# A diffusion block's mixture of experts: large experts' first products from split weights, the other experts' sums ahead of the last weights, the last two experts joined by products

## The chip, the cores and the metric

One core of a Trainium2 chip runs the whole kernel in one launch. The metric is device time in microseconds (us) of an execution. Where a text names an engine: PE is TensorE, DVE is VectorE, ACT is ScalarE, POOL is GpSimd, and SP is SyncE, which here only issues transfers.

## The reference, cut

512 latent tokens of width 1024 and 256 context tokens pass one layer: a mixer (neighbourhood attention and a gated DeltaNet, merged), then a mixture of experts, then a last RMSNorm. The change lies almost wholly in the second half:

```
logits = xf @ w_router + b_router                 # xf: 512 x 1024, modulated RMSNorm of x
top_val, top_idx = top_k(logits, 4)               # 4 of 32 experts for a token
gates = softmax(top_val)
...
hb = xb @ w1[e] + b1[e]                           # w1[e]: 1024 x 2048
gate, up = hb[:, :1024], hb[:, 1024:]
gate = minimum(gate, 7); up = clip(up, -7, 7)
act = (up + 1) * gate * sigmoid(1.702 * gate)
y = act @ w2[e] + b2[e]                           # w2[e]: 1024 x 1024
...
x = x + g2 * sum over the 4 experts of gate * y
out = rmsnorm(x, final_norm_w)
```

Everything is float32. The weights of the experts are 32 x 12 MB (of 2^20 bytes), each read once.

## The kernel before, in words

The first 727 us or so are the mixer. Its projections already work with split operands: a helper (lines 29 and 30 of the profile) copies a float32 tile on ACT to fp32r as the high part and subtracts it on DVE for the low part, and three fp32r products (lines 981, 982 and 984: high by high, low by high, high by low) stand for one in fp32.

For the experts, the router counts each expert's tokens, `order` ranks the experts by count into the row `eint`, and the experts are then worked through by rank. A large one has 128 slots for tokens, a small one 64; with 64 slots the two halves of the 1024 output columns are worked on side by side by the two halves of TensorE's columns. Expert 0 and 1 are large and fixed (their indices are known without the ranking), then even ones are large and odd ones small; the last two, 30 and 31, are small. Tokens beyond an expert's slots go to `overflow`, a loop under a condition at the end, which has nothing to do with these inputs; its condition still joins all engines.

`Stream` loads the weights in 1 MB chunks of 128 partitions x 2048 columns on SP's queue, in a fixed order: for each e the four chunks "g" (gate half of w1) of e, the four of w2 of e - 1, and the four "u" (up half) of e. There are RAWB buffers of the tile "raw"; `pump` issues loads as long as there is room and, beyond the fixed experts, only once `eint` is there.

The loop follows the same order. `mm` makes the products of one such group in fp32 (line 481; one fp32 product of 128x512 shows as two records) and adds the bias by a product (lines 491 and 494). `gate` and `up` make the activation from PSUM on DVE and ACT, `transp` turns it by products with the identity (line 228), `weighted` (line 539) multiplies w2's result by gates and g2, and `scatter` (line 528) writes its rows by an indirect DMA to the DRAM tensor y4d, which has four rows for each token. `fetch` (line 220) loads a later expert's token rows from h2d by an indirect DMA, and `gather` turns them. Experts 0 and 1 get their rows by one-hot products in `slots`. `places` and `overflow_table` make the tables of tokens, rows and gates by one-hot products.

```
def mm(x, e, kind, after=None):
    ...
    for c in range(4):
        r = stream.take(e, kind, c)
        for j in range(2):
            ...
                nc.tensor.matmul(o[n], x[:, k, 0:m], r[:, j, 512 * n:512 * n + 512], ...)
        stream.pump()
```

The tail, after the condition's join: y4d is loaded in 8 transfers of 1 MB (line 84) into the same buffers; DVE (line 611) and POOL (line 621) add them into x1; expert 31's result is added by products with a one-hot matrix (line 706), with the second bias (line 703); squares on ACT (line 713), inverse roots on POOL and DVE, and the stores (line 720).

The order of instructions on an engine is the scheduler's: by the order of the program, but work that is ready can be put ahead, unless `keep_in_program_order` holds it.

Of the kernel before, what the change touches and what calls it, by code (L numbers as in the profile page):

```python
# [18 lines left out]
RAWB = 14  # L19
FIXED = 2  # L20
# [18 lines left out]
class Stream:  # L39
# [3 lines left out]
    def __init__(self, tc, ctx, w1, w2, y4d, NE):  # L43
# [15 lines left out]
        self.tail = False  # L59
# [12 lines left out]
    def pump(self, most=RAWB, behind=None):  # L72
        while self.loaded < min(self.used + most, len(self.order) if self.tail else self.last):
# [21 lines left out]
def small(e):  # L95

    return e >= 30 or e > 1 and e % 2 == 1


def column(e):  # L100

    if e < FIXED:
        return e
    return 61 - e if e >= 30 else 16 + (e - 3) // 2 if e % 2 else e // 2 + 1
# [38 lines left out]
def moe(tc, ctx, cst, release, rps, rt, rtp, h2, hx, h2d, x1d, modd, w1, b1, w2, b2, fn_d, out, NE=32):  # L143
# [5 lines left out]
    y4d = dr.tile([2048, 1024], F32, name="y4d")  # L149
# [4 lines left out]
    pctx = ExitStack()  # L154
    ident, iot, iot1, pcol, ones1 = cst["ident"], cst["iota"], cst["iota1"], cst["pcol"], cst["ones_row"]
    mx, E, cnt = rt.mx, rt.E, rt.cnt

# [36 lines left out]
    def slots():  # L194

        oh = xp.tile([128, 4, 256], F32R, name="yy", bufs=2)
        v = oh.rearrange("p t (a s) -> p t a s", a=2)
        for t in range(4):
            nc.vector.tensor_tensor(v[:, t], iot1[:, None, :].to_broadcast([128, 2, 128]),
                                    rt.pp[:, t, 0:2, None].to_broadcast([128, 2, 128]), op=OP.is_equal)  # L200
        for e in range(2):
            XT[e] = xp.tile([128, 8, 128], F32, name="xt", bufs=3)
        for q in range(4):
            p = bank("tr")
            for b in range(2):
                for i in range(2):
                    for t in range(4):
                        nc.tensor.matmul(p[:, 256 * b:256 * b + 256], h2[i][:, t, 256 * q + 128 * b:256 * q + 128 * b + 128], oh[:, t, :],
                                         start=b == 0 and i == 0 and t == 0, stop=b == 1 and i == 1 and t == 3)
            p = p.rearrange("p (b e s) -> p b e s", b=2, e=2)  # L210
            nc.scalar.activation(XT[0][:, 2 * q:2 * q + 2], p[:, :, 0], AF.Copy)
            nc.vector.tensor_copy(XT[1][:, 2 * q:2 * q + 2], p[:, :, 1])
# [10 lines left out]

    def turn(e, src, q, dst):

        p = bank("tr").rearrange("p (k s) -> p k s", k=4)
        for k in range(4):
            nc.tensor.transpose(p[:, k, :], src[:, (4 * q + k) * 128:(4 * q + k + 1) * 128], ident)  # L228
        if small(e):
            nc.scalar.activation(dst.rearrange("p (n k) s -> p k n s", n=2), p.rearrange("p k (n s) -> p k n s", n=2), AF.Copy)  # L230
        else:
            nc.scalar.activation(dst[:, 4 * q:4 * q + 4], p, AF.Copy)  # L232
# [5 lines left out]
    def gather(e):  # L238
        XT[e] = xp.tile([128, 8, 128], F32, name="xt", bufs=3)
        if small(e):  # L240
            XT[e] = XT[e][:, 0:4].rearrange("p a (b s) -> p (a b) s", b=2)
        turned(e, xg[:, e % 4], XT[e])
# [8 lines left out]
    def order(get):  # L251

        cmp = get([128, 32, 32], BF, 1)
        nc.vector.tensor_scalar(kb, iot[:, 0:32], -1.0, 31.0, op0=OP.mult, op1=OP.add)
        nc.vector.memset(kb[:, 0:1], 1.0e6)
        nc.vector.memset(kb[:, 1:2], 9.0e5)
# [19 lines left out]
    tlast = sb.tile([128, 4], F32, name="tlast")  # L276
# [7 lines left out]
    nc.sync.dma_start(g2b, dap(modd, 3072, [[0, 128], [1, 1024]]))  # L284
    for n in range(2):
        nc.sync.dma_start(g2s[64 * n:64 * n + 64, :], dap(modd, 3072 + 512 * n, [[0, 64], [1, 512]]))
# [36 lines left out]
    def sums(get, pl, sel, n):  # L323

        oh = get([128, 16, 128], BF, 0)
        for i in range(16):
            nc.gpsimd.tensor_scalar(oh[:, i], iot1, pl[:, i:i + 1], None, op0=OP.is_equal)
        rh = get([128, 16, 5, n], BF, 1)
        nc.gpsimd.tensor_tensor(rh[:, :, 0, :], sel, iot[:, 1:17, None].to_broadcast([128, 16, n]), op=OP.mult)
        nc.vector.tensor_scalar(rh[:, :, 1, :], sel, pcol, None, op0=OP.mult)  # L330
        for i in range(3):
            nc.gpsimd.tensor_tensor(rh[:, :, 2 + i, :], sel, gp[:, i, :, None].to_broadcast([128, 16, n]), op=OP.mult)
        return oh, rh

    get = scratch()
    slots()
    order(get)
# [7 lines left out]
    def places():  # L345
# [17 lines left out]
        nc.gpsimd.tensor_tensor(tmp.rearrange("p (t k) e -> p t k e", k=4), E.rearrange("p (t k) e -> p t k e", k=4),  # L363
# [4 lines left out]
        def finish():  # L368
# [9 lines left out]
            nc.vector.tensor_copy(tlast[:, 0:1], toks[:, column(NE - 1):column(NE - 1) + 1])  # L378
# [86 lines left out]
    BS = {}  # L465


    def mm(x, e, kind, after=None):
# [6 lines left out]
        m = 64 if s else 128  # L475
        for c in range(4):
            r = stream.take(e, kind, c)
            for j in range(2):
                k = 2 * c + j
                for n in range(2):  # L480
                    nc.tensor.matmul(o[n], x[:, k, 0:m], r[:, j, 512 * n:512 * n + 512], start=k == 0, stop=w2_ and k == 7)  # L481
            stream.pump()
            if after:
                after(c)
        if not w2_:
            i = 0 if kind == "g" else 1
            if s:
                if kind == "g":
                    BS[e] = wk3.tile([128, 2, 64], F32R, name="bsel", bufs=2)
                    nc.scalar.activation(BS[e], selr[:, :, k0:k0 + 1].to_broadcast([128, 2, 64]), AF.Copy)  # L490
                nc.tensor.matmul(p[0], BS[e].rearrange("p n s -> p (n s)"), bb[:, i], start=False, stop=True)  # L491
            else:
                for n in range(2):
                    nc.tensor.matmul(p[n], selr[:, n, k0:k0 + 1].to_broadcast([128, 128]), bb[:, i], start=False, stop=True)  # L494
# [4 lines left out]
    def gate(e, p):  # L499
        s = wk3.tile([128, 1024], F32, name="sg", bufs=2)  # L500
        for n, b in enumerate(p):
            v = slice(512 * n, 512 * n + 512)
            nc.vector.tensor_scalar(b, b, 7.0, None, op0=OP.min)  # L503
            nc.scalar.activation(s[:, v], b, AF.Sigmoid, scale=1.702)  # L504
            nc.vector.tensor_tensor(s[:, v], s[:, v], b, op=OP.mult)
        GS[e] = s

    def up(e, p):
        s = GS.pop(e)
        for n, b in enumerate(p):  # L510
            v = slice(512 * n, 512 * n + 512)
            nc.vector.tensor_scalar(b, b, 7.0, -7.0, op0=OP.min, op1=OP.max)  # L512
            nc.vector.scalar_tensor_tensor(s[:, v], b, 1.0, s[:, v], op0=OP.add, op1=OP.mult)
        AT[e] = s

    def transp(e):
# [3 lines left out]
        turned(e, AT.pop(e), t)  # L520
        TA[e] = t
# [12 lines left out]
    def weighted(e, p):  # L534
        y = xp.tile([128, 1024], F32, name="yy", bufs=2)
        k = column(e)
        for n, b in enumerate(p):
            v = slice(512 * n, 512 * n + 512)
            nc.vector.scalar_tensor_tensor(y[:, v], b, gates[:, k:k + 1], g2s if small(e) else g2b[:, v], op0=OP.mult, op1=OP.mult)  # L539
        return y[:, 0:512] if small(e) else y  # L540

    def overflow(n, ovi, rowd, gatd):

        with tc.If(n > 0):
            with tc.For_i(0, n) as j:
                e = nc.values_load(ovi[0:1, bass.ds(j, 1)], min_val=0, max_val=31)
                with ExitStack() as s2:
# [57 lines left out]
                    nc.gpsimd.indirect_dma_start(out=y4d[:, :], out_offset=bass.IndirectOffsetOnAxis(ap=rw[:, 0:1], axis=0),  # L605
                                                 in_=y, in_offset=None, bounds_check=2047, oob_is_err=False)

    Y4 = {}

    def add(t, y_, v=slice(0, 1024)):  # L610
        tc.keep_in_program_order(nc.vector.tensor_tensor(x1[:, t, v], x1[:, t, v], y_, op=OP.add))  # L611

    def others(t, c):

        Y4[t, c] = r = stream.take(t, "y", c)
        if t == 3 and c == 0:
# [1260 lines left out]
```

## Time and profile before

| | |
|---|---|
| three runs | 1869.14, 1871.02, 1864.0 us; median 1869.14 |
| the profiled execution | 1867.78 us, its span in the trace 1866.0 us |
| mean granted TensorE clock of it | 0.978 |
| PE busy | 1748.1 us, 94% of the span |
| DVE, ACT, POOL busy | 687.6, 395.4, 267.5 us |
| moved by DMA | 566.05 MB, 303 GB/s over the span |

The span goes from the first to the last record of the trace; 1.8 us of the execution lie around it. A clock of 1.00 in a window is 2.4 GHz, 0.50 is 1.2 GHz. "DMA share" is the mean busy share of the 16 transfer engines.

### The profile page before, as it was taken

How to read it: one execution, taken by the hardware profiler on the slowest of the kernel's cores; microseconds unless marked ns; L12 is line 12 of the kernel's file. 1: busy time of each engine (PE TensorE's matmuls, PEld its weight loads, DVE VectorE, ACT ScalarE, POOL GpSimd, SP SyncE). 2: the span in 40 equal slices, each digit the busy share in tenths (PEclk: the TensorE clock that was granted, in tenths of full speed). 3: DMA queues.
4: the chain of work that ended last, by engine and by line, in shares of the span. 5: the costliest groups of instructions: out<-in, count | busy, mean ns of one | idle time of the engine just before them, and what ended most of it. 6: DMA issues, size and time to landing. Idle time of an engine off the chain costs nothing. (4 is left out here: it accounts for less than half of the span.)

```text
span 1866.0 us, 23887 instructions
## 1 busy us (share of the span) xinstructions
PE 1748.1 (94%) x9003; PEld 955.9 (51%) x9003; DVE 687.6 (37%) x1356; ACT 395.4 (21%) x718; POOL 267.5 (14%) x321
## 2 busy tenths in 40 slices
PE   5979899899989898999999999999999999999984
PEld 1556677777867776444444444444444444444331
DVE  2456796964558766511111111111111111111125
ACT  2534446342246432100000100000000000010001
POOL 0131101433000532340000000000000000000005
PEclk9989899999989998999999999999999999999997
DMA  7647649755785735999999999999999999999995
GB/s 255 206 126 231 206 120 244 185 146 145 190 204 159 241 106 195 394 408 390 373 397 387 406 384 385 403 387 380 400 387 381 389 395 378 375 394 378 404 373 225
DMA packets 263451, 566.05 MB, mean 303 GB/s; under 512 B 61521, under 2 KB 124453, under 8 KB 263204
## 3 DMA queue, kind: packets, MB, share of 16 engines
q1 hardware_dynamic: 186568, 491.26, 72.1%
q10 hardware_dynamic: 69885, 57.00, 10.6%
q0 software_dynamic: 6880, 16.24, 2.3%
q8 instruction: 72, 1.18, 0.3%
q14 instruction: 46, 0.38, 0.1%
HBM read 529.16 MB, written 43.16 MB: 307 GB/s over the span
## 5 line engine op out<-in xcount | busy, mean ns | idle before, releaser
L481 PE MATMUL h<-raw,xt 128*64 128x512 f32 (+1 forms) x2048 | 684.4, 596 | 5.2 <-DMA raw<-in_w_dram 5.0
L481 PEld LDWEIGHTS h<-raw,xt 128*64 128x64 f32 (+1 forms) x2048 | 259.3, 163 | 366.6 <-issue 361.5
L481 PE MATMUL y<-raw,at 128*64 128x512 f32 (+1 forms) x1024 | 338.0, 598 | 0.3 <-ACT at L232 0.3
L481 PEld LDWEIGHTS y<-raw,at 128*64 128x64 f32 (+1 forms) x1024 | 132.6, 164 | 187.7 <-issue 185.5
L981 PE MATMUL pj<-hh,whi 128*128 128x512 f32 (+3 forms) x432 | 163.3, 380 | 7.7 <-ACT zb L1166 3.4
L982 PE MATMUL pj<-hl,whi 128*128 128x512 f32 (+3 forms) x432 | 160.7, 375 | 0.0
L984 PE MATMUL pj<-hh,wlo 128*128 128x512 f32 (+3 forms) x432 | 158.6, 376 | 0.0
L503 DVE TENSOR_SCALAR h<-h 128x512 f32<-128x512 f32 x48 | 31.9, 696 | 314.1 <-PE h L494 207.6
L512 DVE TENSOR_SCALAR h<-h 128x512 f32<-128x512 f32 x48 | 31.9, 696 | 294.8 <-PE h L494 198.8
L30 DVE TENSOR_TENSOR wlo<-raw,whi 128x512 fp32r<-128x512 f32 (+1 forms) x105 | 84.5, 808 | 63.9 <-ACT whi L29 63.5
L528 POOL DMA_INDIRECT y4d<-yy,rows x32 | 32.1, 1003 | 523.4 <-DVE yy L539 522.6
L29 ACT ACTIVATE whi<-raw 128x512 fp32r<-128x512 f32 (+1 forms) x105 | 65.1, 626 | 159.7 <-PE pj L982 71.6
L981 PEld LDWEIGHTS pj<-hh,whi 128*128 128x128 f32 (+1 forms) x432 | 81.8, 189 | 32.8 <-issue 5.4
L220 POOL DMA_INDIRECT A<-h2d,toks x30 | 31.1, 1036 | 425.2 <-PE tr L228 397.8
L982 PEld LDWEIGHTS pj<-hl,whi 128*128 128x128 f32 (+1 forms) x432 | 81.9, 190 | 14.6 <-issue 1.2
L539 DVE SCALAR_TENSOR_TENSOR yy<-y,gates,g2b 128x512 f32<-128x512 f32 x32 | 24.0, 750 | 177.0 <-PE y L481 175.2
L984 PEld LDWEIGHTS pj<-hh,wlo 128*128 128x128 f32 (+1 forms) x432 | 80.3, 189 | 16.0 <-DVE wlo L30 1.4
L232 ACT ACTIVATE at<-tr 128x512 f32<-128x512 f32 x32 | 17.7, 596 | 324.0 <-PE tr L228 324.0
L504 ACT ACTIVATE sg<-h 128x512 f32<-128x512 f32 x48 | 28.3, 597 | 145.6 <-DVE h L503 145.6
L490 ACT ACTIVATE bsel<-selr 128x128 fp32r<-128x128 f32 x16 | 4.8, 307 | 246.5 <-PE h L491 235.4
L1174 DVE SCALAR_TENSOR_TENSOR cv<-zb,cols,cv 128x772 f32<-128x772 f32 (+1 forms) x48 | 45.5, 951 | 4.0 <-ACT cv L1172 3.6
L232 ACT ACTIVATE xt<-tr 128x512 f32<-128x512 f32 x28 | 16.3, 595 | 119.6 <-PE tr L228 119.6
(474 smaller groups left out, 2054.1 us busy)
## 6 DMA issues: line engine op xcount, KB each, us to landing
raw<-in_w_dram SPq DMA_DIRECT2D x384, 1024.0 KB
raw<-in_w_in_dram ACTq DMA_DIRECT2D x44, 512.0 KB
raw<-in_w_mod_dram ACTq DMA_DIRECT2D x32, 512.0 KB
raw<-in_w_mod_dram SPq DMA_DIRECT2D x16, 512.0 KB
raw<-y4d SPq DMA_DIRECT2D x8, 1024.0 KB
kk<-nkd SPq DMA_DIRECT2D x16, 384.0 KB
gad<-st ACTq DMA_DIRECT2D x16, 256.0 KB
raw<-in_w_out_dram ACTq DMA_DIRECT2D x8, 512.0 KB
```

The costliest lines, as they stand in the source:

```text
L29: nc.scalar.activation(hi, src, AF.Copy)
L30: nc.vector.tensor_tensor(lo, src, hi.bitcast(F32), op=OP.subtract)
L220: nc.gpsimd.indirect_dma_start(out=dst, out_offset=None, in_=src, in_offset=bass.IndirectOffsetOnAxis(ap=toks[:, k:k + 1], axis=0), bounds ...
L232: nc.scalar.activation(dst[:, 4 * q:4 * q + 4], p, AF.Copy)
L481: nc.tensor.matmul(o[n], x[:, k, 0:m], r[:, j, 512 * n:512 * n + 512], start=k == 0, stop=w2_ and k == 7)
L503: nc.vector.tensor_scalar(b, b, 7.0, None, op0=OP.min)
L512: nc.vector.tensor_scalar(b, b, 7.0, -7.0, op0=OP.min, op1=OP.max)
L528: s = nc.gpsimd.indirect_dma_start(out=dst, out_offset=bass.IndirectOffsetOnAxis(ap=rows[:, k:k + 1], axis=0), in_=y, in_offset=None, boun ...
L981: nc.tensor.matmul(p, h, mh(k), start=k == 0, stop=False)
L982: nc.tensor.matmul(p, h, ml(k), start=False, stop=False)
L984: nc.tensor.matmul(p, l, mh(k), start=False, stop=k == kb - 1)
L1174: nc.vector.scalar_tensor_tensor(y[:, :n], z[:, t:t + n], taps[:, t, fb:fb + 1], y[:, :n], op0=OP.mult, op1=OP.add)
```

## The change

- `RAWB` goes from 14 to 10 and `FIXED` from 2 to 1. Large are now 0 and the odd experts, small the even ones from 2 and 31.
- Large experts from 5 on (13 of them) make their first products, "g" and "u", from split weights. For each chunk `prep` copies it on ACT to fp32r ("whi", two buffers) and subtracts on DVE ("wlo", two halves of a tile); `mm` then makes three fp32r products for each fp32 one. The first two chunks of a group are prepared ahead, the others two chunks ahead in `mm`. The tokens are split by `gather` in the same way.
- From expert 2 on PE, ACT and DVE keep the order of the program.
- `order` comes ahead of `slots`; `slots` makes expert 0's rows alone, by products with token rows as the moving side, and turns them. Expert 1 is fetched by DMA.
- The one-hot work of the tables goes from POOL to DVE.
- y4d is zeroed in the mixer: eight DMAs of 128 x 17 pieces of 480 bytes and one of 128 x 256 bytes on SP's queue.
- y4d's eight loads stand in the stream's order ahead of the last four chunks of w2, and their rows are added into x1 (three DVE adds and one POOL add for each quarter of the tokens) ahead of the condition's join. Experts 30 and 31 are not scattered: their results, the second bias and x1 itself (by the identity) are summed in PSUM by products; squares are taken from PSUM, and the tail multiplies on DVE.
- The final norm's weights are loaded early and scaled on POOL.

```
-RAWB = 14
-FIXED = 2
+RAWB = 10
+FIXED = 1
...
-        self.last = len(self.order)
-        self.order += [(t, "y", c) for t in range(4) for c in range(2)]
+        self.order[-4:-4] = [(t, "y", c) for t in range(4) for c in range(2)]
...
-    return e >= 30 or e > 1 and e % 2 == 1
+    return e == 31 or e > 0 and e % 2 == 0
...
     def slots():
...
+        oh = wk3.tile([128, 4, 128], F32R, name="oh", bufs=2)
         for t in range(4):
...
+            nc.vector.tensor_scalar(oh[:, t], iot1, rt.pp[:, t, 0:1], None, op0=OP.is_equal)
+        x = xp.tile([128, 1024], F32, name="yy", bufs=2)
+        for n in range(2):
+            p = bank("y")
+            for i in range(2):
+                for t in range(4):
+                    nc.tensor.matmul(p, oh[:, t, :], h2[i][:, t, 512 * n:512 * n + 512], start=i == 0 and t == 0, stop=i == 1 and t == 3)
+            (nc.scalar.copy, nc.vector.tensor_copy)[n](x[:, 512 * n:512 * n + 512], p)
+        gather(0, x)
...
+    def split_(e):
+
+        return not small(e) and e >= 5
+
+    def parts(hi, lo, src):
+        ACT.activation(hi, src, AF.Copy)
+        DVE.tensor_tensor(lo, src, hi.bitcast(F32), op=OP.subtract)
...
+    order(areas([xp.tile([128, 1024], F32, name="yy", bufs=2)]))
+    slots()
     get = scratch()
-    slots()
-    order(get)
...
+    def prep(e, kind, c):
+
+        r = stream.take(e, kind, c)
+        h = wk.tile([128, 2, 1024], F32R, name="whi", bufs=2)
+        l = wlo[:, 2 * (NL[0] % 2):2 * (NL[0] % 2) + 2]
+        NL[0] += 1
+        parts(h, l, r)
+        stream.pump()
+        PRE[e, kind, c] = h, l
+
+    def ahead(e, kind):
+        if e < NE and split_(e):
+            for c in range(2):
+                prep(e, kind, c)
...
+            if len(x) > 1:
+                h, l = PRE.pop((e, kind, c))
+                for a, b in ((x[0], h), (x[1], h), (x[0], l)):
+                    for j in range(2):
+                        k = 2 * c + j
+                        for n in range(2):
+                            PE.matmul(o[n], a[:, k], b[:, j, 512 * n:512 * n + 512], start=k == 0 and a is x[0] and b is h, stop=False)
+                if c < 2:
+                    prep(e, kind, c + 2)
...
+            p = mm(XT[e], e, "g", transposes if e else None)
...
+            gate(e, p)
+            ahead(e, "u")
...
+        pu = mm(XT.pop(e), e, "u", (lambda c: gather(nxt) if c == 1 else None) if nxt else None)
+        ahead(e + 1, "g")
+        up(e, pu)
...
+    transp(NE - 1)
+    strict[0] = False
+    for t in range(4):
+        r = [stream.take(t, "y", c) for c in range(2)]
+        nc.gpsimd.tensor_tensor(r[1][:, 0], r[1][:, 0], r[1][:, 1], op=OP.add)
+        for q in (r[0][:, 0], r[0][:, 1], r[1][:, 0]):
+            nc.vector.tensor_tensor(x1[:, t], x1[:, t], q, op=OP.add)
+        stream.pump()
+    xctx.close()
+    pctx.close()
+    overflow(*ovt)
...
     for t in range(3):
+        second(t)
         last(t, 0)
...
+    p = mm(TA.pop(NE - 1), NE - 1, "w2", early)
+    weighted(NE - 1, p, yl[1])
     for t in range(3):
         last(t, 1)
...
+        squares(t)
+    second(3)
+    rest(3)
     for i in range(2):
         last(3, i)
...
+    squares(3)
+    for t in range(4):
+        final(t)
...
+    for i in range(8):
+        nc.sync.dma_start(dap(y4d, i * 2040, [[16384, 128], [120, 17], [1, 120]]), cst["zero"][:, None, :].to_broadcast([128, 17, 120]))
+    nc.sync.dma_start(dap(y4d, 16320, [[16384, 128], [1, 64]]), cst["zero"][:, 0:64])
     ptd = dr.tile([2, 512, 512], F32, name="ptd")
```

In it `second(t)` makes the bias products of quarter t, `last(t, i)` adds expert 30 + i by its one-hot matrix, and `rest(t)` adds x1 by the identity (called in `early`, after the third chunk of the last w2).

## Rows read from the trace of the kernel before

**Rows 1.** The page, 40 slices of 46.65 us: PE's busy tenths, GB/s:

```profile
PE   5979899899989898999999999999999999999984
...
GB/s 255 206 126 231 206 120 244 185 146 145 190 204 159 241 106 195 394 408 390 373 397 387 406 384 385 403 387 380 400 387 381 389 395 378 375 394 378 404 373 225
```

**Rows 2.** Windows of the experts: length, PE, PEld, DVE, ACT, POOL, clock, DMA share, GB/s:

```profile
737.00:1817.00 1080.00, 1073.49 (x3584) 450.49 (x3584) 189.66 (x319) 87.19 (x160) 96.23 (x106) 1.00 1.01 390
900.00:1700.00 800.00, 799.69 (x2643) 333.04 (x2642) 120.14 (x179) 65.03 (x120) 46.70 (x46) 1.00 1.01 387
1745.00:1796.00 51.00, 51.00 (x200) 18.10 (x200) 7.80 (x11) 2.10 (x4) 1.94 (x2) 1.00 1.03 409
```

**Rows 3.** Waits of PE, 740 to 1866 us: total us, times, longest:

```profile
PE h L481 <- DMA raw<-in_w_dram: 3.6, 3, 1.7
```

**Rows 4.** Timeline of PE in a pair of experts: start, us, what:

```profile
1200.31 1.09 PE L228 MATMUL tr<-ident,sg 128*128 128x128 f32 x8
...
1242.78 7.09 PE L481 MATMUL y<-raw,at 128*64 128x512 f32 x32
...
1267.77 1.09 PE L228 MATMUL tr<-ident,sg 128*128 128x128 f32 x8
```

**Rows 5.** Groups by form, 740 to 1866 us: busy us, mean ns of one:

```profile
L481 PE MATMUL h<-raw,xt 128*128 128x512 f32 x1021 | 450.0, 594 | 0.2 <-ACT xt L232 0.2
...
L611 DVE TENSOR_TENSOR A<-A,raw 128x1024 f32<-128x1024 f32 x9 | 17.4, 1931 | 12.8 <-DMA raw<-y4d 8.0 <-POOL raw L621 4.7
...
L621 POOL TENSOR_TENSOR raw<-raw 128x1024 f32<-128x1024 f32 x5 | 14.5, 2925 | 12.3 <-DMA raw<-y4d 12.3
```

**Rows 6.** Timeline of PE, fp32r products in the mixer:

```profile
208.17 0.39 PE L982 MATMUL pj<-hl,whi 128*128 128x512 f32 x1
...
210.92 0.39 PE L982 MATMUL pj<-hl,whi 128*128 128x512 f32 x1
```

**Rows 7.** Line 29's instructions, the high parts: ns min/median/max:

```profile
L29 ACT ACTIVATE woh<-raw x8: 1040/1045/1059, 614.4 to 661.0; 128x1024 fp32r<-128x1024 f32 x8
```

**Rows 8.** Line 30's instructions, the low parts: ns min/median/max:

```profile
L30 DVE TENSOR_TENSOR wol<-raw,woh x8: 1207/1982/3324, 616.2 to 662.9; 128x1024 fp32r<-128x1024 f32 x8
```

**Rows 9.** Timeline of the experts' start:

```profile
727.59 0.58 SPq L689 DMA_DIRECT2D fnb<-in_final_norm_w_dram  x1
...
738.28 3.67 PE L481 MATMUL h<-raw,xt 128*128 128x512 f32 x8 [1.43 <-DMA raw<-in_w_dram]
...
752.80 0.55 DVE L265 CAST eint<-eidx 1x32 int32<-1x32 f32 x1
```

**Rows 10.** DMA queues, 225 to 258 us: packets, MB, share of 16 engines:

```profile
q10 hardware_dynamic: 3128, 1.58, 17.6%
```

**Rows 11.** Timeline of SP's queue at the start:

```profile
7.11 30.30 SPq L907 DMA_DIRECT2D raw<-in_w_mod_dram  x16
83.72 1.58 SPq L1132 DMA_DIRECT2D gld<-gl  x2
```

**Rows 12.** Windows of the mixer's start, columns as in rows 2:

```profile
37.00:84.00 47.00, 41.77 (x230) 21.65 (x229) 15.63 (x36) 25.96 (x44) 4.90 (x16) 1.00 0.67 214
84.00:106.00 22.00, 21.16 (x127) 16.56 (x126) 11.35 (x15) 8.75 (x15) 12.45 (x46) 1.00 0.43 128
```

**Rows 13.** DMA queues, 281 to 287 us:

```profile
q1 hardware_dynamic: 1984, 0.75, 54.5%
```

**Rows 14.** Timeline of the tail:

```profile
1818.09 1.08 PE L228 MATMUL tr<-ident,sg 128*128 128x128 f32 x4 [2.19 <-DVEq L544]
...
1837.82 3.78 PE L706 MATMUL h<-yl,ohT 64*128 64x512 f32 x8 [7.30 <-DVE yl L726]
...
1859.52 0.15 DVE L753 TENSOR_SCALAR ssf<-ssf 128x1 f32<-128x1 f32 x1
...
1861.24 0.75 DVE L755 TENSOR_SCALAR A<-raw,ssf 128x1024 f32<-128x1024 f32 x1
```

**Rows 15.** Window behind the join, columns as in rows 2:

```profile
1818.00:1824.80 6.80, 6.71 (x19) 3.34 (x21) 0.00 (x0) 0.60 (x1) 0.00 (x0) 0.50 0.48 183
```

More of the change, by code (lines that the diff above doesn't have):

```diff
@@ L72, in pump @@
     def pump(self, most=RAWB, behind=None):
-        while self.loaded < min(self.used + most, len(self.order) if self.tail else self.last):
+        while self.loaded < min(self.used + most, len(self.order)):
             e, kind, c = self.order[self.loaded]
@@ L475, in mm @@
         m = 64 if s else 128
+        if s and kind == "g":
+            BS[e] = wk3.tile([128, 2, 64], F32R, name="bsel", bufs=2)
+            ACT.activation(BS[e], selr[:, :, k0:k0 + 1].to_broadcast([128, 2, 64]), AF.Copy)
         for c in range(4):
[L477 to L482, printed above, removed]
+            if len(x) > 1:
[7 more added lines that the diff above has]
+                    prep(e, kind, c + 2)
+            else:
+                r = stream.take(e, kind, c)
+                for j in range(2):
+                    k = 2 * c + j
+                    for n in range(2):
+                        PE.matmul(o[n], x[0][:, k, 0:m], r[:, j, 512 * n:512 * n + 512], start=k == 0, stop=w2_ and k == 7)
+                stream.pump()
             if after:
@@ L604, in overflow @@
                         nc.vector.scalar_tensor_tensor(y[:, v], p, ga, g2b[:, v], op0=OP.mult, op1=OP.mult)
[L605 to L616, printed above, removed]
-            for i in range(2):
-                for n in range(2):
-                    nc.tensor.matmul(LP[t, n], ident, r[:, i, 512 * n:512 * n + 512], start=False, stop=i == 1)
-        elif t < 3 and (c == 1 or t > 0):
-            nc.gpsimd.tensor_tensor(r[:, 0], r[:, 0], r[:, 1], op=OP.add)
-            add(t, r[:, 0])
-        else:
-            for i in range(2):
-                add(t, r[:, i])
-        stream.pump()
+                    tf = lp.tile([128, 4], F32, name="tf")
@@ new lines, in moe, with second, last, rest @@
+    LP = {}
+    def second(t):
+        for n in range(2):
+            LP[t, n] = bank(("h", "h", "tr", "y")[t])
+            PE.matmul(LP[t, n], Gt[:, 128 * t:128 * t + 128], bs[:, 512 * n:512 * n + 512], start=True, stop=False)
+    def last(t, i):
+        for n in range(2):
+            h = slice(64 * n, 64 * n + 64)
+            PE.matmul(LP[t, n], ohT[i][h, t, :], yl[i][h, :], start=False, stop=i == 1)
+    def rest(t):
+        for n in range(2):
+            PE.matmul(LP[t, n], ident, x1[:, t, 512 * n:512 * n + 512], start=False, stop=False)
@@ L675, in moe @@
[L675 to L689 removed]
+            ohT = [wk3.tile([128, 4, 128], F32, name="oh", bufs=2) for _ in range(2)]
@@ new lines, in squares, with final @@
+    def squares(t):
+        for n in range(2):
+            ACT.activation(junk[:, 512 * n:512 * n + 512], LP[t, n], AF.Square, accum_out=sq[:, n, t:t + 1])
+    def final(t):
+        v = slice(t, t + 1)
+        DVE.tensor_tensor(ss[:, 0, v], sq[:, 0, v], sq[:, 1, v], op=OP.add)
+        DVE.tensor_scalar(ss[:, 1, v], ss[:, 0, v], 1.0 / 1024, 1e-6, op0=OP.mult, op1=OP.add)
+        rsqrt1(nc, ss[:, 2, v], ss[:, 1, v], ss[:, 0, v])
+        for n in range(2):
+            c = slice(512 * n, 512 * n + 512)
+            nc.vector.scalar_tensor_tensor(xf[:, t, c], LP[t, n], ss[:, 2, v], fnb[:, c], op0=OP.mult, op1=OP.mult)
+        nc.sync.dma_start(out.rearrange("o (t p) d -> (o t) p d", p=128)[t], xf[:, t])
@@ L761, in moe @@
+    for t in range(4):
+        final(t)
     pctx.close()
+    wctx.close()
     inner.close()
```

275 lines of the change are left out of this document (116 added, 159 removed).

## Prediction

> **What bounds the kernel now.** I read the page's forty slices first: from slice 17 (about 750 us) to the end the PE digits are all 9 and the bytes run at 373 to 408 GB/s, so three fifths of the span are the experts and two resources are nearly full in it at once [rows 1]. Which of them sets the pace is told by the windows: between 900 and 1700 us TensorE is busy for 799.69 of 800 us at a clock of 1.00, while the transfers carry 387 GB/s; in 51 us near the end, where the stream had more free buffers, they carried 409 [rows 2]. The waits agree: in all the experts TensorE waits only 3.6 us for weights [rows 3]. So TensorE is the bound, but the stream is 387/409, 95%, of the best rate seen behind it. A pair of experts, one large and one small, repeats every 1267.77 - 1200.31 = 67.46 us [rows 4]; at 387 GB/s that is 26.1 MB, which takes 64.1 us at 407 GB/s (I take 407, just under the 409 and at the better slices). Whatever TensorE gains beyond 3.4 us in a pair, the stream doesn't follow.
>
> **The split products.** The first products of a large expert are 32 fp32 products of 128x512; the groups show 1021 records in 450.0 us, two records to a product, 0.88 us a product or 28.1 us for an expert's 32 [rows 5]. An fp32r product of this shape runs in the mixer: from 208.17 to 210.92 there are 12 starts, 0.229 us each [rows 6]. Three of them are 0.69 us, so 32 x 0.69 = 22.0 us: TensorE saves some 5.3 to 6 us for each of the 13 split experts, and its pair falls to about 62 us. That is under the stream's 64.1: the bound changes hands, by 2 us in a pair. If TensorE alone counted, 13 x 5.5 = 72 us would go; the stream leaves 13 x 3.4 = 44 us of it.
>
> **Making the parts.** Each 1 MB chunk (2048 columns) of a split expert needs an ACT copy and a DVE subtraction. In the mixer 1024 columns take 1.045 us on ACT [rows 7] and at least 1.207 us on DVE [rows 8]; doubled, 2.1 and 2.4 us. A chunk's 12 products take 2.75 us. Two buffers of parts exist and each chunk is made two ahead, so the two engines work beside each other and beside the products; for one pair that is 8 x 2.4 = 19 us on DVE, beside its small load now (120 of 800 us [rows 2]). I cost it at nothing. Cover: the 2.75 us of products over each chunk, with 0.35 us to spare on DVE; without it 2.1 + 2.4 = 4.5 us a chunk come in series (a rival, below). The program order held on PE, ACT and DVE puts an expert's last step of up behind two preps, but the transposes that need it stand behind two chunks of the next product; nothing there is late by more than these cover.
>
> **The stream, to the landing of the last "u" chunk.** From 737 to 1817 us, 1080 us at 390 GB/s, 421.2 MB moved [rows 2]. Without the last expert's w2 (4.2 MB, now later) and two scatters no longer made (0.4 MB) that is 416.6 MB; at 407 it takes 1023.6 us, to 1760.6. What the stream loses on the way: ordering the experts now stands ahead of expert 0's rows on DVE, and its rows are transposed after being picked. Ordering ended at 752.80 us while TensorE had begun its products at 738.28 [rows 9]; put ahead, it and the transposes delay the first product by 4 to 10 us. The stream itself isn't held by that, having expert 0's eight chunks to load first. Then experts 0, 1 and 3 keep fp32 products, 3.5 us for a chunk against 2.6 us of loading, with 10 buffers instead of 14: TensorE paces the stream until expert 5. Bounds: nothing (the stock carries it) and 16 us (some 56 chunks up to expert 5 at TensorE's pace, less ten in stock). I take 10, so the last "u" chunk lands at 1770.6 us.
>
> **The zero fill.** New on the SP queue, ahead of the experts by far: 8 DMAs of 2176 pieces of 480 bytes, 17408 pieces. Loads in 512-byte pieces took 17.6% of 16 engines over 33 us for 3128, which is 29.7 ns each [rows 10]; so 17408 x 29.7 / 16 = 32 us of all the engines. A store far down the program is issued as soon as it can be: the load of the final norm's weights, one of the last lines, stood at 727.59 us, ahead of the experts' weights [rows 9]. So I expect it at the start, where SP issues the modulation weights until 37.4 us and then nothing until 83.72 [rows 11]. From 37 to 84 us the engines are busy 0.67, from 84 to 106 us 0.43 [rows 12]: 47 x 0.33 + 22 x 0.57 = 28 us of room. Nearly all hides if it lies there; if it runs while the modulation or input weights are awaited, all 32 us count. Bounds 0 and 32; I take 8, by the room.
>
> By the Trainium skill, page "DMA: Bandwidth & Descriptors", section "Specifications", a transfer needs pieces of at least 512 bytes for the line rate, and below that the engine reads, changes and writes back. By that the fill would hold the engines 65 us, an estimate; a row of 128-byte writes shows no such penalty: 1984 pieces in 54.5% of 6 us, 26 ns each [rows 13].
>
> **The tail.** The eight loads of y4d (8.4 MB) now stand ahead of the last w2: 20.6 us, to 1791.2; the last w2 lands 10.3 us later, at 1801.5. The last quarter's sum is one POOL add (2.925 us) and one DVE add (1.2 to 1.9) [rows 5]: 1795.5. The join of all engines, behind which TensorE waited 2.19 us before [rows 14], I put at 1.8: 1797.3. TensorE has by then idled since the last "u" product, some 20 us. Before, after that much shorter wait, its clock was 0.50 (1.2 GHz) for 6.8 us [rows 15]; I take the same 6.8, to 1804.1. In it fit the six bias products (fp32r, 0.23 us at full speed [rows 6], so some 0.5 at half) and two of the three pairs of expert 30's products at 1.7 us (eight records in 3.78 us [rows 14]); the third takes 0.9. From 1805.0 at full speed: w2's 32 records as in the pair [rows 4], 7.1, and six identity products of 0.86, 5.1: 1817.2. Weighting, by a DVE step of 0.75 [rows 14], 1.1 with its handoffs; three pairs of expert 31, 0.86 each, 2.6; the last quarter's bias, identity and two pairs, 0.5 + 1.7 + 1.7; squares on ACT 1.6: 1826.4. The inverse root's small DVE steps, 1859.52 to 1861.24 before [rows 14], 1.7, and two DVE steps of 0.75: 1829.6. From the end of the last DVE step, 1861.24 + 0.75 [rows 14], to the span's end before, 1866.0, were 4.0 us for the store: 1833.6. With the zero fill's 8: a span of 1841.6. The profiled execution was 1867.78 us with a span of 1866.0, 1.8 around it: **1843 us**. That execution stands 1.4 us under the median of the runs, 1869.14, which I leave.
>
> Moving the one-hot work from POOL to DVE, the earlier load of the norm's weights (0.5 MB, POOL scales it in idle time), and gathering expert 1 by DMA cost nothing that I can place: DVE has 680 us free in 800, and the loads are in the bytes. Expert 1's fetch stands behind expert 0's table, and 28 us of fp32 products cover it; without the cover some 5 us.
>
> **The rivals.**
> B, the fill hides wholly, the start loses nothing, the rate is 409: 1843 - 8 - 10 - 5 = 1820 us. For it, the room of 28 us; against, the slower consumption up to expert 5.
> C, the fill lies wholly on the start's path: 1843 + 24 = 1867 us, no change. For it, PE and ACT do wait for weights there; against, the idle engines.
> D, the change doesn't do what it says, because the stream's ceiling is the 387 GB/s it has now and 409 was a short burst: the stretch takes 1076 us instead of 1024, y4d 1 us more: about 1893 us, slower. For it, the DMA share is already 1.01 at 387 [rows 2]; against, 51 us at 409 with two scatters in them. It decides below 0.397, where 26 us over 1055 are lost.
> E, the parts set the pace: ACT and DVE in series, 4.5 us a chunk, 36 us for an expert's eight instead of 28.1; 13 x 8 = 103 us on TensorE's side, and the sums of y4d then hide behind it (about 20 us): some 1950 us. It decides from about 3.5 us a chunk, TensorE's pace now. For it, the subtraction took up to 3.3 us in the mixer [rows 8]; against, two buffers and two engines.
> F, the small pieces cost double: 65 us; with a quarter of it showing 1851, with all of it 1900.
>
> **How the numbers follow.** Likeliest A 0.58, its own range 1825 to 1860 (the fill and the start's bounds); B 0.12; C 0.10; D 0.08; E 0.08; F 0.04. The range leaves out D, E and most of F, 0.19: 1812 to 1872. A difference under 0.5% (9.3 us) can't be told from none here. Faster than 1859.8: nearly all of A, B and a little of F, 0.68; within: C, the top of A and a mild D, 0.14; slower 0.18.
>
> **What would show it.** The experts' windows at 400 to 409 GB/s with TensorE now waiting for weights or parts, pairs near 64 us; fp32r products at 0.23 us; preps of 2.1 and 2.4 us; the last "u" chunk near 1770; the fill before 106 us; TensorE at 0.50 after the join. Wrong: pairs near 67 with the share at 1.01 (D); TensorE waiting for DVE in every split chunk (E); the mixer longer by 20 us or more (C, F).

## The result, and the profile after

The changed kernel takes 1889.45 us (median of four runs, 1888.94 to 1890.3) against 1868.94 for the kernel before: a ratio of 1.0114, 95% interval 1.0094 to 1.0134. The forecast was 1843, faster, with a range up to 1872: wrong in sign, and outside the range. The profiled execution took 1889.57 us with a span of 1887.5.

In the page's slices of the changed kernel (PE's busy tenths, the granted clock in tenths, GB/s) the experts run at 398 to 409 GB/s from slice 21 on, but for one slice at 359 and the last one, where they had 373 to 408 before [rows 1]; the start and the end look worse:

```profile
PE   1798799999989988899999999999999999999666
...
PEclk7898999999999999899999999999999999999887
...
GB/s 283 280 128 174 247 108 236 203 134 163 148 213 195 198 157 134 389 302 378 388 405 409 409 409 409 408 407 406 401 400 402 407 399 398 408 405 399 359 404 77
```

The time line of PE gives three landmarks: the last product of the routing, the first expert product, and the bias product that ends the last expert's "u".

```profile
757.19 0.27 PE L136 MATMUL rt<-M,ones_bf 128*128 128x32 bf16 x4 [2.33 <-DVE pp L133]
...
764.98 10.46 PE L165 MATMUL h<-raw,xth 128*128 128x512 f32 x24
...
1820.38 0.51 PE L165 MATMUL h<-bb,bsel 128*128 128x512 f32 x1
```

(In the changed kernel a wrapper issues most of the experts' instructions, so that they stand under its one line, 165.) Before, the same landmarks were at 726.86, 738.28 and 1815.40. Cut there, the whole difference of the two spans is accounted for:

| | before | forecast | after |
|---|---|---|---|
| to the end of the routing | 726.9 | +8.0 | +30.3 |
| from there to the end of the last "u" | 1088.5 | -42.8 | -25.3 |
| from there to the end of the span | 50.6 | +10.4 | +16.5 |
| span | 1866.0 | -24.4 | +21.5 |

(The forecast's column is its own sum: 8 for the fill; the last "u" product's bias some 2 us behind its weights at 1778.6; the rest to 1841.6.) The change does win in the middle, but less than forecast, and both ends lose.

**The start.** SP's queue in the changed kernel, time line:

```profile
7.88 5.74 SPq L948 DMA_DIRECT2D raw<-in_w_mod_dram  x4
13.73 30.03 SPq L1339 DMA_DIRECT2D y4d<-zero  x8
43.81 3.86 SPq L1340 DMA_DIRECT2D y4d<-zero  x1
47.77 17.39 SPq L948 DMA_DIRECT2D raw<-in_w_mod_dram  x12
```

The fill isn't behind the modulation weights, as expected from [rows 11], but between the fourth and the fifth of their sixteen loads, and the other twelve stand behind it. TensorE waits for these weights (us in total, times, longest):

```profile
PE dn L949 <- DMA raw<-in_w_mod_dram: 39.2, 9, 29.3
```

The windows of the same stretches (length, PE, PEld, DVE, ACT, POOL, clock, DMA share, GB/s) show it starved; before, from 37 to 84 us, it was busy for 41.77 us [rows 12]:

```profile
0.00:37.00 37.00, 9.38 (x33) 1.98 (x33) 9.40 (x29) 9.23 (x16) 2.04 (x9) 0.86 0.98 287
37.00:84.00 47.00, 25.63 (x112) 7.16 (x112) 5.15 (x10) 10.43 (x17) 0.00 (x0) 0.78 0.89 278
```

**The middle.** The stream by windows:

```profile
753.70:948.69 194.99, 184.79 (x621) 83.62 (x621) 63.17 (x180) 22.61 (x36) 26.81 (x19) 0.96 0.98 364
948.69:1740.00 791.31, 777.83 (x3141) 417.56 (x3140) 365.41 (x311) 254.12 (x224) 77.14 (x45) 1.00 1.02 405
1740.00:1800.00 60.00, 44.57 (x168) 21.75 (x168) 20.70 (x21) 9.17 (x11) 6.13 (x3) 0.89 1.00 365
1800.00:1844.00 44.00, 21.51 (x100) 7.21 (x96) 24.74 (x17) 1.79 (x3) 10.85 (x4) 0.79 1.01 402
```

Where experts are split the stream carries 405 GB/s where it had 387 [rows 2], and ACT, which makes the high parts, waits for weights. In the waits of ACT (us in total, times, longest) and the groups of the same stretch:

```profile
ACT whi L165 <- DMA raw<-in_w_dram: 90.7, 68, 4.6
```

```profile
L165 DVE TENSOR_TENSOR B<-raw,whi 128x2048 fp32r<-128x2048 f32 x101 | 229.8, 2289 | 162.0 <-ACT whi L165 161.9
L165 ACT ACTIVATE whi<-raw 128x2048 fp32r<-128x2048 f32 x101 | 192.9, 1915 | 117.8 <-DMA raw<-in_w_dram 90.7 <-PE h L165 26.3 <-DVE sg L165 0.6
```

The parts of a chunk cost 1.92 us on ACT and 2.29 on DVE (2.1 and 2.4 forecast), and TensorE hardly waits for them: 7.2 and 6.2 us in all. Its longest waits from 725 us on:

```profile
PE h L165 <- DVEq L596: 21.0, 1, 21.0
PE tr L424 <- DVE yy L421: 15.2, 1, 15.2
PE h L165 <- DVE B L165: 7.2, 26, 0.5
PE h L165 <- ACT whi L165: 6.2, 10, 1.3
```

The second of them, 15.2 us at 1760, was in no step of the prediction: the second bias's preparation was there before too, but now PE keeps the order of the program, and the transposes that wait for that preparation hold the next expert's products. A pair takes 65.65 us instead of the 67.46 of [rows 4]:

```profile
1238.73 1.09 PE L165 MATMUL tr<-ident,sg 128*128 128x128 f32 x8
...
1304.38 1.09 PE L165 MATMUL tr<-ident,sg 128*128 128x128 f32 x8
```

**The end.** Windows between the end of "u" and the join, behind the join, and in the last steps on DVE:

```profile
1820.90:1845.00 24.10, 0.63 (x4) 0.42 (x4) 23.48 (x14) 0.60 (x1) 10.85 (x4) 0.60 0.96 384
...
1845.00:1853.80 8.80, 8.72 (x18) 3.02 (x18) 0.00 (x0) 0.00 (x0) 0.00 (x0) 0.54 0.06 23
...
1872.00:1883.20 11.20, 2.47 (x10) 0.69 (x8) 10.16 (x35) 1.39 (x6) 0.00 (x0) 0.72 0.35 141
```

DVE sums y4d for nearly all of the 24 us (12 adds) while TensorE waits; then TensorE works for 8.8 us at a clock of 0.54, against 6.8 at 0.50 in [rows 15]; and the last multiplications go through DVE one quarter at a time, a chain of some 3.2 us each.

### The profile page after: what moved, and what is told of

The parts are those of the page before. It is cut to its first block, busy times and chain, and to the rows that moved or that the text cites. A ratio compares the mean times of both kernels' runs of the same rounds, so it can differ in the third digit from the quotient of the medians.

```text
span 1887.5 us, 25145 instructions
## 1 busy us (share of the span) xinstructions
PE 1702.2 (90%) x9411; PEld 1031.8 (55%) x9411; DVE 952.7 (50%) x1555; ACT 590.6 (31%) x829; POOL 261.7 (14%) x251
## 3 DMA queue, kind: packets, MB, share of 16 engines
q10 hardware_dynamic: 69885, 57.00, 10.4%
## 5 line engine op out<-in xcount | busy, mean ns | idle before, releaser
L165 PE MATMUL y<-raw,at 128*128 128x512 f32 (+1 forms) x1024 | 336.9, 595 | 0.0
L165 DVE TENSOR_TENSOR B<-raw,whi 128x2048 fp32r<-128x2048 f32 x104 | 236.6, 2289 | 162.3 <-ACT whi L165 162.2
L165 ACT ACTIVATE whi<-raw 128x2048 fp32r<-128x2048 f32 x104 | 198.6, 1915 | 119.1 <-DMA raw<-in_w_dram 92.0
L165 PEld LDWEIGHTS y<-raw,at 128*128 128x128 f32 (+1 forms) x1024 | 132.8, 164 | 186.0 <-issue 185.3
L165 PE MATMUL h<-raw,xts 128*64 128x512 f32 x1024 | 233.3, 598 | 0.0
L165 PE MATMUL h<-whi,xth 128*128 128x512 f32 x416 | 118.1, 406 | 6.4 <-ACT whi L165 6.2
L165 PE MATMUL h<-B,xth 128*128 128x512 f32 x416 | 116.1, 401 | 7.2 <-DVE B L165 7.2
L165 PE MATMUL h<-whi,xtl 128*128 128x512 f32 x416 | 113.8, 395 | 0.0
L165 PEld LDWEIGHTS h<-B,xth 128*128 128x128 f32 x416 | 75.8, 188 | 35.9 <-DVE B L165 19.8
L165 PEld LDWEIGHTS h<-whi,xth 128*128 128x128 f32 x416 | 74.7, 188 | 34.1 <-ACT whi L165 17.7
```

Source lines behind the costliest of these rows:

```text
L165: i = f(*a, **k)
```

## Experiments

Theories: **S**, the stream of weights sets the pace from expert 5 on, so TensorE's gain there can't be had in full, and the fill's time at the start is lost beside it; against it **T**, TensorE (or the making of parts) still sets the pace. For the fill: **place** (it costs because the modulation weights stand behind it) against **time** (its 32 us of all engines are paid wherever it lies). Each ratio below is to the kernel before, run on the same chip; a microsecond figure is the difference of two ratios times 1867.

**e1_zero_rows**: no fill; zero rows for the last two experts by scatter. It leaves out the rows of the overflow slots, which these inputs don't use.

```
-    for i in range(8):
-        nc.sync.dma_start(dap(y4d, i * 2040, [[16384, 128], [120, 17], [1, 120]]), ...)
-    nc.sync.dma_start(dap(y4d, 16320, ...), cst["zero"][:, 0:64])
...
             ovt = ovt()
+            z = xp.tile([128, 1024], F32, name="yy", bufs=2)
+            nc.gpsimd.memset(z[:, 0:512], 0.0)
+            for i in (NE - 2, NE - 1):
+                scatter(i, z[:, 0:512])
```

> The changed kernel without the zero fill; instead the rows of the last two experts alone are zeroed by two small scatters during expert 3, as the kernel before did for one expert (overflow rows, of which these inputs have none, are left unwritten). If the fill costs because 32 us of engine time stand ahead of the modulation weights, the first expert product comes some 25 to 30 us earlier (about 737 instead of 765) and the time is about 1860 us. If the later start of the experts has another cause (the new order of ranking and picking), the time stays within 5 us of the changed kernel's 1889.

Measured: 1859.58 us, ratio 0.9954 (0.9934 to 0.9974), 30 us under the changed kernel. The routing ends at 731.52 and the first expert product comes at 739.96, 25 us earlier: of the 26.7 us by which the changed kernel was later there than the kernel before, 1.7 are left. The rest is no more than profiles without the fill differ by among themselves (the routing ends at 731.52 in e1, 724.38 in e8, 732.18 in e9 and 725.54 in e9b). So the fill is the start's loss, and without it the change is already a little faster than the kernel before.

**e2_fill_gap** and **e3_fill_mid**: the fill where it was expected, and in the emptiest place of the mixer.

```
+    issue_behind(tc, d.ins, WL.ins)       # e2: WL is the last load of w_mod on SP
...
+    issue_behind(tc, d.ins, LH[0])        # e3: LH[0] is the last store of the keys; fill emitted there
```

> The same fill, its DMAs held behind the last modulation-weight load on SP's queue, which is where the prediction put it (its room of 28 us between 37 and 106 us). If the place is what costs, nearly all hides: 1862 to 1868 us. If the engine time is paid wherever it lies, because the input weights then queue behind it, about 1889 us.

> The same fill, held behind the last store of the keys on SP's queue, at about 250 us, where a window of 20 us of the changed kernel has the DMA engines at a share of 0.20. If only the place costs: 1858 to 1864 us, as without the fill. If the engine time is paid anywhere: about 1889 us.

Measured: e2 1905.15 us, ratio 1.0194 (1.0142 to 1.0246), 15 us slower than the changed kernel; e3 1879.93 us, 1.0075 (1.0052 to 1.0099), 7 us faster, though the intervals just touch, and 23 slower than e1. Neither hides it. In e2's time line of ACT, three small loads (2 KB each) that ACT issues one behind the other lie 20 us apart, first to last, while the fill runs. The activation behind them, which makes the input projection's operands, comes at 61.85 us, where it came at 45.78 in the kernel before; its 46.53 us are all the time that ACT had been idle, nearly half of it ahead of the fill:

```profile
41.52 20.28 ACTq L1063 DMA_DIRECT2D raw<-in_b_mod_dram  x3
...
61.85 1.45 ACT L987 ACTIVATE h<-pj,msh,msc 128x512 f32<-128x512 f32 x2 [46.53 <-DMA y4d<-zero]
```

Taken one by one, each of the three is issued in about 0.25 us; the time lies between them:

```profile
41.52 0.27 ACTq L1063 DMA_DIRECT2D raw<-in_b_mod_dram  x1
...
57.77 0.26 ACTq L1063 DMA_DIRECT2D raw<-in_b_mod_dram  x1
...
61.57 0.24 ACTq L1063 DMA_DIRECT2D raw<-in_b_mod_dram  x1
```

What ACT waits for is in the trace's semaphores: the program gives eight completion semaphores in turn to the transfers of SP and of ACT alike. The second load's semaphore was last given to the fill's fourth transfer, which landed at 57.62 us, and the third's to the fill's fifth, which landed at 61.49. So two loads of 2 KB each stood behind 1 MB of zeros, and ACT's work behind the loads. The routing ended at 774.18 us, 42.7 later than in e1; the part of it that isn't ACT's 16 us wasn't singled out.

In e3 the window of the fill, first without it (e1) and then with it:

```profile
200.00:260.00 60.00, 56.87 (x348) 47.05 (x348) 53.34 (x122) 24.24 (x43) 4.59 (x4) 1.00 0.43 134
```

```profile
200.00:260.00 60.00, 47.28 (x257) 38.13 (x255) 41.01 (x94) 18.78 (x33) 4.60 (x4) 0.89 0.97 250
```

At a share of 0.43 the engines had 34 us to spare in these 60, about what the fill needs; yet PE lost 9.6 us and DVE 12.3, and the routing ended at 745.05 instead of 731.52. The same wait shows: two small stores of ACT, of 2 KB each, were issued at 233.46 and 241.19, right behind the landings of the two fill transfers that had their semaphores (233.44 and 241.16), and ACT's next activations had waited

```profile
233.78 0.63 ACT L1233 ACTIVATE w<-kq 128x512 f32<-128x512 f32 x1 [6.25 <-DMA y4d<-zero]
...
241.45 0.39 ACT L1209 ACTIVATE zb<-pj 128x256 f32<-128x256 f32 x1 [6.52 <-DMA y4d<-zero]
```

12.8 us together, against the 13.5 that the routing lost. So "place" holds only in part, and the idle share of the engines says little here: ACT's short transfers waited for the bulk ones. No run gives them semaphores of their own, so what would be left of the cost then isn't shown.

**e4_no_split** and **e5_high_only**: no split at all, and splits of which only the first product is made.

```
-        return not small(e) and e >= 5
+        return False                                        # e4
...
-                for a, b in ((x[0], h), (x[1], h), (x[0], l)):
+                for a, b in ((x[0], h),):                   # e5
```

> The changed kernel with no expert split: all first products in fp32, all else as it is. If the stream of weights sets the pace with the split (64.4 us a pair) and TensorE without it (67.5 us), the last first product ends some 40 us later, the sums of y4d then hide behind it, and the time is 1905 to 1925 us. If TensorE set the pace in both, it is 72 us slower, 1960 us. If the split gains nothing, 1889 us.

> The changed kernel with only the first of the three products (high part by high part) of each split product; the two with a low part are left out, so the result is less exact. TensorE's work in a split expert falls by another 64 x 0.23 = 14.7 us. If the stream sets the pace, only the stream's dips can be won: it runs at 409 GB/s instead of 402 from 949 to 1844 us, 15 us less: 1874 to 1886 us. If TensorE set the pace, 13 x 14.7 = 191 us less: about 1700 us.

Measured: e4 1920.11 us, ratio 1.0271 (1.0233 to 1.0309), 29 us slower than the changed kernel; e5 1886.1 us, 1.0116 (1.0092 to 1.0139), no different from it. The windows of e4, then e5:

```profile
949.00:1740.00 791.00, 791.00 (x2604) 329.64 (x2603) 120.84 (x177) 63.62 (x119) 44.94 (x44) 1.00 1.01 389
```

```profile
949.00:1740.00 791.00, 667.79 (x2332) 305.84 (x2333) 361.40 (x309) 253.76 (x223) 78.37 (x45) 0.90 1.02 405
```

Without the split TensorE is busy for all of it and the stream carries 389. With two thirds of the split products gone, TensorE is idle for 123 us of 791, and the stream carries 405 as with all of them, and the kernel ends at the same time. S holds; T, which gave 1700 us for e5, falls. (e5 still makes all the parts; that their making doesn't set the pace is read from the waits above, ACT's for weights and TensorE's for parts.)

**e6_bias_apart**: the second bias's preparation taken apart, so that no product waits for it.

```
+        yield          # in second_bias: behind the loads, behind DVE's steps, at the end
...
+            next(sbias)    # at expert 30's start, behind its up step, behind its w2
```

> The changed kernel with the second bias's preparation for the tail (which held TensorE for 15.2 us at 1760) taken apart: its loads stay, its POOL, ACT and DVE steps come after expert 30's up step, its transposes after expert 30's w2. If the stream sets the pace, only what it lost at that place comes back (365 GB/s for 60 us instead of 405: 6 us): 1883 to 1888 us. If the stall is on the path that sets the end: 15 us less, 1874 us.

Measured: 1886.66 us, ratio 1.0112 (1.0084 to 1.0139): the changed kernel's own ratio. The wait of 15.2 us is gone and the stream carries 387 GB/s from 1740 to 1800 instead of 365, but 361 instead of 402 in the 44 us behind; TensorE now waits 9.0 us for weights instead, and the end hardly moves. TensorE's stall was not on the path; what the stream lost by it is under what these runs can tell.

**e7_sums_first**: y4d's loads and sums ahead of the last "u".

```
-        self.order[-4:-4] = [(t, "y", c) ...]
+        self.order[-8:-8] = [(t, "y", c) ...]
...                               # and the adds emitted ahead of the last mm(..., "u")
```

> The changed kernel with the loads of y4d and their sums one group earlier, ahead of the last expert's u chunks instead of behind them. The last landing stays where it is (about 1844 us), but the sums then hide behind the last first product, the join comes 2 to 5 us earlier, and TensorE idles some 3 us before it instead of 21, so that its clock may stay up: 4 to 10 us less, 1879 to 1885 us. If the order of the last loads is indifferent: 1889 us. If the sums delay the activation of the last expert on DVE: slower, some 1895 us.

Measured: 1884.37 us, ratio 1.0095 (1.0068 to 1.0123): 4 us less at the middle, but the intervals overlap. In its profile the products behind the join begin at 1844.60 instead of 1845.08, so the join hardly moved. TensorE, which waited 15.87 us for the last "u" weights instead, was as slow behind it; its clock did not stay up, as I had hoped.

**e8_all**: no fill, zero rows for every slot, the bias apart, the sums first, and the inverse roots of three quarters in one chain; **e9_spread** the same with the zero scatters spread over experts 4 to 25; **e9b_spread_only** the changed kernel with the spread scatters in the fill's place and nothing else.

```
+            for j in range(NOV):          # e8: 20 in a row behind the overflow table
+                s = nc.gpsimd.indirect_dma_start(out=y4d[:, :], ... orow[:, j:j + 1] ..., in_=z, ...)
...
+        if 4 <= e < 24:                   # e9, e9b: one slot's two half rows for each expert
+            for i in range(2):
+                s = nc.gpsimd.indirect_dma_start(... OR[0][:, i, e - 4:e - 3] ..., in_=OR[1], ...)
...
-    for t in range(4):
-        final(t)
+    final(0, 3)                           # e8, e9
+    final(3, 4)
```

> All four mends together: no fill, but zero rows scattered for the last two experts and for every overflow slot; the second bias apart; the sums first; and in the tail the inverse roots of three quarters taken together (one chain of small DVE steps instead of three). If the terms add up (30 + 4 + 7 + 2 us): 1843 to 1850 us, faster than the kernel before by about 1%. If the stream only hands a gain of one place to the next: 1858 us, as without the fill alone.

> The four mends again, but the zero rows for the overflow slots are scattered two at a time over experts 4 to 23, and those of the last two experts in 24 and 25, instead of 22 in a row on POOL during expert 3 (28 us, behind which that expert's own scatter and a fetch stood; the stream fell to 319 GB/s between 800 and 900 us against 368 without them, some 12 us). If that row of scatters is what ate the gain: 8 to 12 us less than before this mend, 1855 to 1860 us. If the stream's own limit eats it, because the later pairs only wait for weights anyway: 1864 to 1868 us.

> The changed kernel with the fill replaced by those spread scatters alone (every slot is covered again), nothing else mended. If the fill's engine time is the whole of what the removal gave: as with the two scatters alone, 1858 to 1862 us. If 42 more scatters on POOL cost something themselves: up to 10 us more.

Measured: e8 1867.84 us, ratio 1.0015 (1.0002 to 1.0028), worse than e1; e9 1854.48 us, 0.9936 (0.9918 to 0.9955); e9b 1860.48 us, 0.9974 (0.996 to 0.9987). In e8 the window of the scatters, beside the same one of e9b:

```profile
800.00:900.00 100.00, 93.38 (x307) 38.95 (x305) 16.72 (x33) 6.74 (x13) 28.61 (x29) 0.97 0.87 319
```

```profile
800.00:900.00 100.00, 100.00 (x341) 42.80 (x340) 18.04 (x37) 8.32 (x16) 29.99 (x31) 1.00 1.00 368
```

TensorE lost 6.6 us and the stream 49 GB/s over 100 us, some 12 us; e9 is 15 us faster than e8. I had put it down to the row of 22 scatters on POOL, behind which an expert's own scatter and a fetch stood. The traces don't bear that out: POOL doesn't keep the program's order, and in e9b the scatters that the program spreads run in a row too, with the own scatter and the fetch inside it, at about the same times. The two in e8, then in e9b:

```profile
891.59 0.99 POOL L594 DMA_INDIRECT y4d<-yy,rows  x1 [0.30 <-issue]
892.88 1.04 POOL L228 DMA_INDIRECT A<-h2d,toks  x1 [0.31 <-issue]
```

```profile
889.45 0.98 POOL L586 DMA_INDIRECT y4d<-yy,rows  x1 [0.30 <-issue]
...
897.19 1.05 POOL L228 DMA_INDIRECT A<-h2d,toks  x1 [0.31 <-issue]
```

What e8 alone shows is a stop of the stream and slow products, from about 886 to 897 us, with no cause that the profile names ("issue"):

```profile
885.00:890.00 5.00, 3.19 (x10) 0.68 (x6) 0.69 (x1) 0.16 (x1) 3.90 (x4) 1.00 0.05 0
```

```profile
894.35 1.01 PE L165 MATMUL h<-raw,xts 128*64 128x512 f32 x1 [2.20 <-issue]
```

Its scatters are written for whole rows of y4d, those of e9 and e9b for half rows; what stopped e8 stays open. e9 is the fastest version run: 33 us under the changed kernel and 12 under the kernel before. The three mends besides the fill are worth 7 us of it together (e9 against e9b, 0.9936 and 0.9974, whose intervals just don't touch).

**e11_ten_buffers**: the kernel before with ten buffers.

```
-RAWB = 14
+RAWB = 10
```

> The kernel before with 10 buffers for the stream instead of 14, all else as it is. The prediction charged part of 10 us at the start to the smaller stock. If the number of buffers matters where TensorE sets the pace: 5 to 15 us slower, with waits of TensorE for weights. If ten are as good as fourteen there: within 3 us of the kernel before, and the loss at the start of the changed kernel comes from the order of its experts and its later start.

Measured: 1884.79 us, ratio 1.0089 (1.0072 to 1.0105), 17 us slower. The windows behind the first products, before and then with ten:

```profile
740.00:800.00 60.00, 60.00 (x206) 29.17 (x205) 31.31 (x77) 5.57 (x10) 24.94 (x31) 1.00 1.03 397
```

```profile
740.00:800.00 60.00, 54.68 (x176) 25.25 (x175) 26.09 (x57) 6.32 (x10) 21.86 (x24) 0.94 0.86 302
```

Here the stream has nothing to fill once ten are full, until TensorE gives one back: 95 GB/s less over 60 us is 5.7 MB, 14 us of loading. TensorE falls much less behind. The same bias product at 1600 us, before and then with ten buffers, is 3.1 us later, as all of them are from expert 2 to expert 30; the bias product that ends the last "u" is 14.5 us later:

```profile
1600.53 1.03 PE L494 MATMUL h<-bb,selr 128*128 128x512 f32 x2
...
1815.40 0.49 PE L491 MATMUL h<-bb,bsel 128*128 128x512 f32 x1
```

```profile
1603.61 1.03 PE L494 MATMUL h<-bb,selr 128*128 128x512 f32 x2
...
1829.90 0.50 PE L491 MATMUL h<-bb,bsel 128*128 128x512 f32 x1
```

So the smaller stock costs the stream 14 us at the start but TensorE 3; the rest of the 17 us comes from 1790 us on, in the last expert and the tail. Why it comes there wasn't singled out.

## Why the prediction was wrong, step by step

**What bounds the kernel, and that the bound changes hands: right.** The stream takes over at 405 GB/s (407 forecast) and limits the gain of the split to 29 us (e4), not the 72 that TensorE alone would have given; e5 shows that TensorE's time over the split experts no longer counts. Rival D (a ceiling at 387) falls by the window at 405 (its own sum comes to some 1897, not 1893), and E (parts in series) by 13.4 us of waits for parts in all. The products, the parts and their cover came as costed.

**The zero fill: the step that failed.** It was costed at 8 us "by the room". Its engine time was right: 17408 pieces at [rows 10]'s 29.7 ns gave 32 us, and from 20 to 46 us, where nothing but the fill's pieces moves, the changed kernel's DMA queue reads (packets, MB, share of 16 engines)

```profile
q1 hardware_dynamic: 14498, 6.91, 107.0%
```

30.7 ns a piece, 33 us for all. It kept SP's queue from 13.73 to 47.67. Two assumptions under the room were wrong. It was placed behind the modulation weights because SP was free there; but those loads have four buffers, and from the fifth on they wait for the products that free them. In the kernel before, SP's waits there:

```profile
SPq L907 <- PE dn L908: 17.5, 10, 4.3
```

The fill waited for nothing and came between the fourth load and the fifth. And free share was taken for room: e2 put the fill just there and it cost more, e3 put it in an emptier stretch and two thirds showed, in both with ACT waiting for the fill's own landings. Rival C had the mechanism, with the whole of the fill on the start's path, and got 0.10. Without the fill the kernel lands at 1859.6 (e1), inside the range. F, the doubled price of small pieces, falls by the fill's own 33 us. (The row set against it beforehand was misread: the 1984 records of [rows 13] hold 0.75 MB, 378 bytes each on average, so they aren't all writes of 128 bytes; the 1742 that are of 128 bytes took 14 ns each.)

**The stream's loss at the start: mis-sized.** It was put at 10 us between bounds of 0 and 16. At 364 GB/s for 195 us against 407 it was 195 x 43 / 407 = 20.6 us. The fill has no part in it: e1 carries 365 in its own first 195 us.

```profile
728.00:923.00 195.00, 184.82 (x621) 83.99 (x620) 63.38 (x179) 22.01 (x36) 29.36 (x22) 0.95 0.98 365
```

e11 shows one reason in the kernel before: with ten buffers the stream falls 14 us behind at the first experts. There TensorE set the pace and felt 3 us of it until the last expert; here the stream sets the pace. Another is a cover that failed: expert 1's fetch was put at nothing behind 28 us of products, and TensorE waited for it.

```profile
799.66 1.73 PE L165 MATMUL tr<-ident,A 128*128 128x128 f32 x7 [4.66 <-DMA A<-h2d,toks]
```

How the 20.6 us divide is open. The 4 to 10 us by which the new order was to delay the first product didn't come: it follows the routing's last by 7.8 us, 11.4 before. The dip at the second bias, 365 GB/s for 60 us, is another 6 us of the stream's own time that no step had; that mending it alone shows nothing at the end (e6) leaves it open whether it counts.

**The tail: mechanism right, size off by 6 us.** The sums, the join, the low clock behind it and the order of the products came as said. The slow stretch lasted 8.8 us instead of 6.8, and the last steps of the first three quarters, which the sum had at nothing, weren't hidden under the products of the fourth: the chain on DVE runs from 1869.84 to 1883.17, and from the last squares (1875.83) to its end are 7.3 us, where 3.2 had been counted.

22 us at the start, 17.5 in the middle and 6 at the end make the 46 us between the forecast span and the measured one. No one of them turns the sign by itself: with the first alone the forecast would still be 2 us under the kernel before. But without the first the span would have been 1 us under it instead of 21.5 over.

## What to carry to other kernels

When a product gets cheaper, first divide the bytes of the stage by the best rate that the trace shows: that time, not TensorE's, is the new floor. What the stream loses ahead of that floor (a smaller stock, a late fetch) is then a term of the sum, and it has to be sized. Work that depends on nothing can be issued earlier than its line suggests, so its place must be held by a dependence. An idle share of transfer engines is not yet room: look for who waits for a landing, also through a semaphore that a bulk transfer shares with short ones. Here the fill cost about its whole engine time or more in two places out of three, and doing without it, as e1 and e9 do, was better than any place. And look in the trace whether work spread in the program is spread on the engine.

## What the runs showed of the hardware

- A transfer's issue can hold its queue: a fill transfer of 2176 pieces took 3.79 us of SP's queue (median of eight, changed kernel), a 1 MB load of weights 0.37. ACT's loads of 2 KB took about 0.25 us to issue while the fill ran (e2); what held ACT between them were the fill's landings, awaited on shared semaphores.
- The fill moved 8.4 MB in pieces of 480 bytes at about 270 GB/s, 30.7 ns a piece, close to the 29.7 of the 512-byte loads in [rows 10]. So the rule of the Trainium skill weighed in the prediction (page "DMA: Bandwidth & Descriptors", section "Specifications", reading and writing back below 512 bytes) doesn't show in this case: its 65 us, an estimate, would have been plain.
